# Six scratch tiles, later rope factors, a rearranged first entry and later tails in a four-layer hybrid kernel

## The chip, the cores and the metric

The kernel runs on one core of one Trainium2 chip. The metric is the device time of one execution in microseconds (us); lower is better. The four compute engines are TensorE (PE in the profile, with PEld for its weight loads), VectorE (DVE), ScalarE (ACT) and GpSimd (POOL); SP is the engine whose queue issues the DMAs.

## The reference

One sequence of 16 meta tokens and 1024 tokens, width 1024, passes through four residual layers: sliding-window attention (A), mLSTM (B), HGRN2 (C) and attention again.

```
for i in range(DEPTH):                       # kinds A, B, C, A
    u = rmsnorm(h, norm_gain[i])
    y = branch[i](u)                         # in-projection, mixer, gate, out-projection
    h = h + y

# A: 16 query heads, 4 key/value heads of 64, window of 128, blocks of 128
q, k, v, z = split(u @ w_in, (1024, 256, 256, 1024))
q = rope(rmsnorm(q, q_gain), pos); k = rope(rmsnorm(k, k_gain), pos)
o = sliding_window_attention(q, k, v, sinks)
y = (o * silu(z)) @ w_out

# C: 8 heads, per step of the scan over chunks
o     = (q * exp(A)) @ S + att(q, k, A) @ v
S_new = exp(A_last) * S + (k * exp(A_last - A)).T @ v
```

Everything is float32. A product is made of three products of fp32r parts: a high and a low part of each operand, the low-low product left out.

## The kernel before, in words

Activations lie transposed: width on the partitions in 8 slabs (KT), tokens along the free dimension in three chunks of 400, 384 and 256 columns (`CHUNKS`). `x` is the residual, `uh` and `ul` the high and low part of the normalised input. `proj` multiplies a 128-column weight slab with one chunk in 24 matmuls (8 slabs, three products) into a PSUM tile `pj`.

The program is a list of steps. Each step has a nominal PE cost, and lists are merged by these costs: `weave` mixes two lists in proportion, `later` and `spread` put a step in after so many nanoseconds of nominal PE time. That fixes PE's order of instructions as written. The other engines' orders are chosen by a scheduler, from readiness and from which buffers are free, and then run in that order. So one more buffer can change the orders of ACT, DVE, POOL and of SP's DMA queue, with PE's left alone.

Three buffers matter. `tmp()` hands out scratch tiles `t` of 128x404 from `TMPS` = 5. The rope factors `cs` (cosine and sine) have a single buffer. The ring `v` has ten tiles of 258 columns.

In the attention layers `qk_proj` handles a chunk of a query or key projection. `evac` copies the PSUM tile to `dst` (L523), squares it into `sq` (L524), and starts four DMAs that write `dst` with its halves swapped into `rot` (L527); `dst`, `sq` and `rot` are three scratch tiles for queries and for the second key slab, and rows of a larger pool for the first key slab. It first issues the DMA of the rope factors (L520). `finish` adds three delayed steps: 2000 ns later `stat`, a matmul of `sq` with a mask (L533) and two ACT steps (L361, L362); 4000 ns later `rope`, four DVE instructions (L538 to L541); 6000 ns later the split into high and low parts: L492 and L493 for queries (`q_split`), L473 to L476 for keys (`k_split`).

Normalisation (`Norm`): the 8 slabs of a chunk are squared on ACT (L377) and added up on DVE (L381), a matmul with a block of ones sums over partitions (L389), ACT forms the reciprocal root, and 8 `unit` steps make `uh` and `ul` (L415, L195, L196). In the first layer this is done chunk by chunk while the first projections run: the sums come in two halves per chunk (`PARTS`), put between the projections at fractions of their time (`FIRST`). Per chunk the head of layer one does a key slab and the first query slab; the second query slab follows for all three chunks after the third.

In layer C each of 8 heads goes through 5 regions of tokens. `level` (DVE and ACT) builds decay factors, `levels_mm` a burst of small matmuls into `pm` (L1127, L1137), `tail0` masks and sums them into `att` (DVE, POOL L1165, ACT). The tail follows while the next region's levels are made: `tail1` transposes (`pt`, L1187), `tail2` for each block does `po` (L1202 with `att`, L1204 with the state `S`) and `pa` (L1209), from which DVE makes the next `S` (L1214). `TAIL_LAG` is the nominal time by which the tail is put back before it is woven with the next region.

```
mx += weave(main[r], last)
last = [[TAIL_LAG, lambda: None, None]] + tails[r]
```

Of the kernel before, what the change touches and what calls it, by code (L numbers as in the profile page):

```python
# [30 lines left out]
    return (0, NMETA) if b == 0 else (NMETA + P * (b - 1), P)  # L31


C_IDENT, C_ONES = 0, 128
C_W = 256
# [76 lines left out]
def hybrid_kernel(ctx: ExitStack, tc: tile.TileContext, ins, out, layers=(0, 1, 2, 3)):  # L112
# [13 lines left out]
    def nm(x):  # L126
        ctr[0] += 1
        return f"{x}{ctr[0]}"
# [10 lines left out]
    def tmp():  # L139
        return tpool.tile([P, 404], F32, tag="t", name=nm("t"), bufs=TMPS)  # L140
# [12 lines left out]

    s.preload_act_table_set("natural_log_exp_and_others")

    const = cpool.tile([P, C_W], F32, name="const")
    ident = const[:, C_IDENT : C_IDENT + P]
    ones = const[:, C_ONES : C_ONES + P]
# [11 lines left out]
    def load_x(n):  # L170
        c0, cn = CHUNKS[n]
        for k in range(KT):
            sp.dma_start(x[:, k, c0 : c0 + cn], ins["xT"][k, :, c0 : c0 + cn])

    load_x(0)
    sp.dma_start(const, ins["const"])
    sp.dma_start(ngain, ins["ngain"])

    layer_pool = [None]
# [189 lines left out]
        return f  # L369

    class Norm:
        def __init__(self, i):
            self.i, self.acc, self.ps = i, {}, {}

        def sq(self, m, n, c0, cn, size=KT):
            q = tmp()[:, :cn]
            s.activation(q, x[:, m, c0 : c0 + cn], AF.Square)  # L377
            if m % size == 0:
                self.acc[n] = q
            else:  # L380
                v.tensor_tensor(self.acc[n], self.acc[n], q, op=ALU.add)  # L381

        def stat(self, n, part=0, parts=1):
            cn = CHUNKS[n][1]
# [7 lines left out]

            return [4 * cn * MM, fn, None]

        def stats(self, n, parts):

            c0, cn = CHUNKS[n]
            size = KT // parts

            def squares(part):  # L400
                def fn():
                    for m in range(part * size, (part + 1) * size):
                        self.sq(m, n, c0, cn, size)

                return [0.0, fn, None]

            return [z for k in range(parts) for z in (squares(k), self.stat(n, k, parts))]

        def unit(self, n, k):
            c0, cn = CHUNKS[n]  # L410
# [34 lines left out]
    def layer_a(i, j, first, last, fin):  # L445
# [69 lines left out]
        def qk_proj(src, gcol, work, fsplit, ch):  # L515
            late = {}

            def evac(acc, n, c0, cn):
                cos_sin = R["mix"].tile([P, 2, 400], F32, tag="cs", name=nm("cs"), bufs=1)
                sp.dma_start(cos_sin[:, :, :cn], ins["rope"][:, :, c0 : c0 + cn].rearrange("a p t -> p a t"))  # L520
                dst, sq, rot = work(n, c0, cn)
                late[n] = dst, sq, rot, cos_sin
                s.activation(dst, acc[:, :cn], AF.Identity, scale=R["cons"][:, gcol : gcol + 1])  # L523
                s.activation(sq, acc[:, :cn], AF.Square)  # L524
                for q in range(4):
                    o = q ^ 1
                    sp.dma_start(rot[32 * q : 32 * q + 32], dst[32 * o : 32 * o + 32])  # L527

            def finish(n, c0, cn):
                def stat():  # L530
                    dst, sq, rot, _ = late[n]
                    st = psa()
                    pe.matmul(st[:, :cn], R["masks"][:, 0:P], sq, start=True, stop=True)  # L533
                    rstd_from(st, sq, cn, 64)

                def rope():
                    dst, sq, rot, cos_sin = late[n]
                    v.tensor_tensor(dst, dst, cos_sin[:, 0, :cn], op=ALU.mult)  # L538
                    v.tensor_tensor(rot, rot, cos_sin[:, 1, :cn], op=ALU.mult)
                    v.tensor_tensor(dst, dst, rot, op=ALU.add)  # L540
                    v.tensor_tensor(dst, dst, sq, op=ALU.mult)  # L541
# [741 lines left out]
        return head, body, oc[5], oc[7]  # L1283

    steps = []
    norm = Norm(layers[0])

    steps += norm.stats(0, PARTS[0]) + [norm.unit(0, k) for k in range(KT)]
    tail = None
    for pos, i in enumerate(layers):  # L1290
        lastl = pos == len(layers) - 1
# [43 lines left out]
    steps[k][2]()  # L1335
    steps[k][2] = None
    load_x(1)
    k = 0
    for n, (cost, fn, pre) in enumerate(steps):
        while k < len(steps) and (k <= n or ahead < LOOKAHEAD):  # L1340
# [29 lines left out]
def _layout(inp):  # L1370
# [4 lines left out]
    const = np.zeros((P, C_W), np.float32)  # L1375
    const[:, C_IDENT : C_IDENT + P] = np.eye(P)
    const[:, C_ONES : C_ONES + P] = 1.0
    am = np.zeros((P, 384), np.float32)
    am[:64, :64] = 1.0
    am[64:, 64:128] = 1.0  # L1380
# [5 lines left out]
    f["const"] = const  # L1386
# [77 lines left out]
```

## Time and profile before

| | before |
|---|---|
| three runs | 2693.47, 2697.60, 2699.81 us |
| the profiled execution, its own time | 2690.46 us |
| its span, first to last instruction | 2688.7 us |
| layer one's entry, up to the first score matmul | 0 to 87 us |
| rest of layer A, then B, C, A | about 87 to 560, to 1560, to 2210, to the end |

A line of the timeline or of a wait names engine, source line, operation, output and inputs. A bracket at its end gives the engine's idle time just before and the instruction that ended it. PE's work is the largest, so an idle gap of PE is the first thing to look for. An idle gap on another engine matters only if PE waits for it.

### The profile page before, as it was taken

The page shows a single profiled execution, that of the slowest core. Times are in us where ns is not written, and L with a number is a line of the kernel's source. Part 1 is how long each engine was busy: PE and PEld are TensorE (multiplying, and loading weights), DVE is VectorE, ACT ScalarE, POOL GpSimd, SP SyncE. Part 2 cuts the span into 40 slices and gives each one's busy share as a digit, 9 for nine tenths or more (in the row PEclk, how much of TensorE's full clock was granted, in tenths as well). Part 3 has the DMA queues.
Part 4 walks back from the last instruction along what each step waited for, and adds up shares of the span by engine and source line. Part 5 has one row for each costly group of instructions (what it writes and reads, how often), then busy time and mean ns, then how long its engine had stood idle before and what let it go on. Part 6 is the DMA issues. An engine that isn't in the chain of part 4 may idle for free.

```text
span 2688.7 us, 54502 instructions
## 1 busy us (share of the span) xinstructions
PE 2590.5 (96%) x20276; PEld 2492.4 (93%) x20276; DVE 1959.5 (73%) x5337; ACT 1693.4 (63%) x4339; POOL 370.1 (14%) x760
## 2 busy tenths in 40 slices
PE   6899999999999999999999999999999998998999
PEld 5898989999999999999999998999999898898999
DVE  7787687974646474747475688978878978886886
ACT  7776777565454545454545657877676857766772
POOL 0343243000000000000000000101000000541450
PEclk8999999999999999999999999999999999999999
DMA  4223111011111111111111111101111013212212
GB/s 148 84 59 96 52 58 46 21 65 56 40 56 40 56 40 56 40 56 40 56 40 53 51 34 33 34 33 34 41 33 39 31 45 107 69 53 88 73 36 75
DMA packets 89786, 145.66 MB, mean 54 GB/s; under 512 B 12448, under 2 KB 42272, under 8 KB 89520
## 3 DMA queue, kind: packets, MB, share of 16 engines
q1 hardware_dynamic: 89520, 142.17, 16.9%
q8 instruction: 160, 2.62, 0.4%
q14 instruction: 106, 0.87, 0.1%
HBM read 127.28 MB, written 4.26 MB: 49 GB/s over the span
## 4 chain that ended last, share of the span: by engine, by line
PE 72%; DVE 12%; ACT 8%; issue 3%; POOL 2%; DMA 2%; SPq 0%; ACTq 0%; DVEq 0%; POOLq 0%
PE pj L262 35%; PE pj L345 14%; PE pj L307 9%; ACT Sm L633 1%; PE po L667 1%; PE pt L648 1%; PE po L890 1%; POOL Sm L637 1%; PE pa L904 1%; PE po L892 1%; DVE t L415 1%; DVE ul L196 1%; DVE Sm L630 1%; DVE x L348 1%; PE pj L303 1%
## 5 line engine op out<-in xcount | busy, mean ns | idle before, releaser
L262 PE MATMUL pj<-uh,wh 128*128 128x256 f32 (+2 forms) x2688 | 930.5, 346 | 3.4 <-ACT uh L195 3.4
L262 PE MATMUL pj<-ul,wh 128*128 128x256 f32 (+2 forms) x2688 | 871.7, 324 | 3.2 <-DVE ul L196 3.1
L262 PE MATMUL pj<-uh,wl 128*128 128x256 f32 (+2 forms) x2688 | 869.6, 324 | 0.0
L262 PEld LDWEIGHTS pj<-uh,wh 128*128 128x128 f32 x2688 | 513.4, 191 | 24.3 <-issue 6.4
L262 PEld LDWEIGHTS pj<-ul,wh 128*128 128x128 f32 x2688 | 513.7, 191 | 15.2 <-DVE ul L196 5.3
L262 PEld LDWEIGHTS pj<-uh,wl 128*128 128x128 f32 x2688 | 513.2, 191 | 0.1
L637 POOL TENSOR_SCALAR Sm<-Sm,s 128x256 f32<-128x256 f32 (+2 forms) x272 | 254.5, 947 | 410.7 <-DVE s L635 406.0
L196 DVE TENSOR_TENSOR wl<-wr,wh 128x512 fp32r<-128x512 f32 x336 | 228.7, 690 | 54.1 <-ACT wh L195 51.8
L195 ACT CAST wh<-wr 128x512 fp32r<-128x512 f32 x336 | 201.9, 616 | 97.9 <-PE pj L345 27.1
L348 DVE TENSOR_TENSOR x<-x,pj 128x384 f32<-128x384 f32 (+2 forms) x480 | 234.7, 510 | 38.8 <-PE pj L345 37.1
L345 PE MATMUL pj<-yh,wh 128*128 128x384 f32 (+2 forms) x768 | 252.9, 329 | 0.0
L345 PE MATMUL pj<-yl,wh 128*128 128x384 f32 (+2 forms) x768 | 248.0, 323 | 3.3 <-DVE yl L196 3.3
L345 PE MATMUL pj<-yh,wl 128*128 128x384 f32 (+2 forms) x768 | 246.6, 321 | 0.0
L307 PE MATMUL pj<-wh,uh 128*128 128x256 f32 x768 | 231.0, 301 | 0.0
L307 PE MATMUL pj<-wh,ul 128*128 128x256 f32 x768 | 216.4, 282 | 0.0
L307 PE MATMUL pj<-wl,uh 128*128 128x256 f32 x768 | 216.1, 281 | 0.0
L633 ACT ACTIVATE Sm<-Sm,s 128x257 f32<-128x257 f32 (+2 forms) x272 | 130.6, 482 | 84.6 <-DVE s L630 75.5
L432 DVE SCALAR_TENSOR_TENSOR t<-pj,t 128x384 f32<-128x384 f32 (+2 forms) x192 | 99.0, 515 | 107.0 <-ACT t L431 106.5
L433 ACT ACTIVATE t<-t 128x384 f32<-128x384 f32 (+2 forms) x240 | 117.8, 491 | 80.1 <-DVE t L432 79.0
L345 PEld LDWEIGHTS pj<-yl,wh 128*128 128x128 f32 x768 | 145.1, 189 | 5.7 <-DVE yl L196 5.2
L195 ACT CAST yh<-r 128x384 fp32r<-128x384 f32 (+2 forms) x120 | 57.3, 479 | 143.8 <-PE pj L345 126.2
L345 PEld LDWEIGHTS pj<-yh,wh 128*128 128x128 f32 x768 | 145.3, 189 | 1.7 <-DVE S L1214 0.3
(235 smaller groups left out, 5470.9 us busy)
## 6 DMA issues: line engine op xcount, KB each, us to landing
wr<-in_b_win SPq DMA_DIRECT2D x128, 256.0 KB, 2.9
wr<-in_a_win SPq DMA_DIRECT2D x80, 256.0 KB, 2.9
wr<-in_c_win SPq DMA_DIRECT2D x64, 256.0 KB, 2.8
cs<-in_rope SPq DMA_DIRECT2D x28, 384.0 KB, 3.3
wr<-in_a_wout SPq DMA_DIRECT2D x32, 256.0 KB, 2.7
wr<-in_b_wout SPq DMA_DIRECT2D x32, 256.0 KB, 2.7
cs<-in_rope SPq DMA_DIRECT2D x20, 256.0 KB, 2.7
t<-t SPq DMA_DIRECT2D x104, 48.0 KB, 2.2
```

The lines of the kernel that those rows point to most:

```text
L195: s.copy(h, src)
L196: v.tensor_tensor(l, src, h.bitcast(F32), op=ALU.subtract)
L262: pe.matmul(acc[:, :cn], a[:, k, :], b[:, k, c0 : c0 + cn], start=(k == 0 and i == 0), stop=(k == KT - 1 and i == 2))
L303: pe.matmul(acc[:48, :256], um[0][:, k, :], m[:, kk, :], start=(k == 0 and m is wh), stop=(k == KT - 1 and m is wl))
L307: pe.matmul(acc[:cn, :256], a[:, k, c0 : c0 + cn], m[:, kk, :], start=(k == 0 and i == 0), stop=(k == KT - 1 and i == 2))
L345: pe.matmul(acc[:, :cn], a[:, k, mc], b, start=(k == 0 and i == 0), stop=(k == 1 and i == 2))
L348: v.tensor_tensor(x[:, m, c0 : c0 + cn], x[:, m, c0 : c0 + cn], acc[:, :cn], op=ALU.add)
L415: v.scalar_tensor_tensor(u, x[:, k, cs], ngain[:, self.i, k : k + 1], self.acc[n], op0=ALU.mult, op1=ALU.mult)
L432: v.scalar_tensor_tensor(a[:, :cn], z, 0.0, a[:, :cn], op0=ALU.min, op1=ALU.subtract)
L433: s.activation(a[:, :cn], a[:, :cn], AF.Exp)
L633: s.activation(Sm[:nq, u, : nk + 1], Sm[:nq, u, : nk + 1], AF.Exp, scale=-1.0, bias=st[:nq, u : u + 1], accum_out=den[:nq, u : u + 1])
L637: g.tensor_scalar(Sm[:nq, u, :nk], Sm[:nq, u, :nk], den[:nq, u : u + 1], None, op0=ALU.mult)
```

## The change

It has five parts.

1. `TMPS` goes from 5 to 6.
2. In `qk_proj` the tile for the rope factors and its DMA move from `evac` into `stat`.
3. `TAIL_LAG` goes from 600 to 2000.
4. The head of layer one does all three projections (key, first and second query slab) for each chunk, so the second query slab no longer comes last.
5. The first norm: for chunk 0 the squares are summed in four parts of two slabs. For chunks 1 and 2 they are summed in one go, the additions on GpSimd and the sum in a row of its own; the places of these steps are new. The block of ones is written by a memset, and the identity is loaded later by its own DMA. In all layers the sum of squares of chunk 2 lies in the `v` ring and no longer in a scratch tile.

```diff
-TAIL_LAG = 600.0
+TAIL_LAG = 2000.0
-ROWS, TMPS, RAWS, YS = 8, 5, 2, 3
+ROWS, TMPS, RAWS, YS = 8, 6, 2, 3
-PARTS = 2, 2, 2
-FIRST = 0.3, 0.9, 0.3, 0.7
+PARTS = 4
+FIRST = (0.2, 0.8, 0.85), (0.2, 0.75, 0.8)
...
+    ones = cpool.tile([P, P], F32, name="ones")
+    v.memset(ones, 1.0)
...
-    sp.dma_start(const, ins["const"])
...
         def sq(self, m, n, c0, cn, size=KT):
-            q = tmp()[:, :cn]
+            if m % size:
+                q = tmp()[:, :cn]
+            elif self.row is not None and n:
+                q = self.row[:, c0 : c0 + cn]
+            else:
+                q = (vtile() if n == 2 else tmp())[:, :cn]
             s.activation(q, x[:, m, c0 : c0 + cn], AF.Square)
             if m % size == 0:
                 self.acc[n] = q
             else:
-                v.tensor_tensor(self.acc[n], self.acc[n], q, op=ALU.add)
+                (v if self.row is None or n == 0 else g).tensor_tensor(self.acc[n], self.acc[n], q, op=ALU.add)
...
             def evac(acc, n, c0, cn):
-                cos_sin = R["mix"].tile([P, 2, 400], F32, tag="cs", name=nm("cs"), bufs=1)
-                sp.dma_start(cos_sin[:, :, :cn], ins["rope"][:, :, c0 : c0 + cn].rearrange("a p t -> p a t"))
                 dst, sq, rot = work(n, c0, cn)
...
                 def stat():
-                    dst, sq, rot, _ = late[n]
+                    dst, sq, rot = late[n]
+                    cos_sin = R["mix"].tile([P, 2, 400], F32, tag="cs", name=nm("cs"), bufs=1)
+                    sp.dma_start(cos_sin[:, :, :cn], ins["rope"][:, :, c0 : c0 + cn].rearrange("a p t -> p a t"))
+                    late[n] = dst, sq, rot, cos_sin
...
-            if n == 2:
+            if first:
+                parts += [tile_of([qb[0][n]], [qb[1][n]])]
+            elif n == 2:
                 parts += [tile_of(*qb)]
...
-    norm = Norm(layers[0])
-    steps += norm.stats(0, PARTS[0]) + [norm.unit(0, k) for k in range(KT)]
+    norm = Norm(layers[0], row())
+    for k in range(PARTS):
+        steps += [norm.squares(0, k, PARTS), norm.stat(0, k, PARTS)]
+    steps += [norm.unit(0, k) for k in range(KT)]
...
-            for n, t0, t1, end in ((2, h0 + h1 * FIRST[2], h0 + h1 * FIRST[3], h0 + h1), (1, h0 * FIRST[0], h0 * FIRST[1], h0)):
-                st = norm.stats(n, PARTS[n])
-                later(seq, *((t0 + (t1 - t0) * k / len(st), z) for k, z in enumerate(st)), *norm.units(n, t1, end))
+            for n, t, h in ((2, h0, h1), (1, 0.0, h0)):
+                t0, t1, t2 = (t + z * h for z in FIRST[n - 1])
+                later(seq, (t0, norm.squares(n)), (t1, norm.stat(n)), *norm.units(n, t2, t + h))
```

Lines of the new kernel are numbered a little differently: the squares L377 are L379, the DVE and GpSimd additions L383, the copies L523 and L524 are L519 and L520, the key split L471 to L474, the stat matmul L532, layer C's `po` L1203 and L1205, `pa` L1210.

First place, the entry. On DVE before, in the stretch where chunk 1 is normalised, the additions of the squares (L381) stand between the weight splits (`wl`) and the first unit (L415):

```order
L381 TENSOR_TENSOR t_218<-t_218,t_220 128x384
L381 TENSOR_TENSOR t_218<-t_218,t_223 128x384
L381 TENSOR_TENSOR t_218<-t_218,t_226 128x384
L381 TENSOR_TENSOR t_243<-t_243,t_245 128x384
L381 TENSOR_TENSOR t_243<-t_243,t_248 128x384
L196 TENSOR_TENSOR wl_384<-wr_385,wh_383 128x512
L381 TENSOR_TENSOR t_243<-t_243,t_251 128x384
L196 TENSOR_TENSOR wl_384<-wr_389,wh_383 128x512
L415 SCALAR_TENSOR_TENSOR t_274<-x,ngain,t_243 128x384
```

On POOL now, at the start of its program, the seven additions for chunk 1 into the row `r_95`, one after the other, with some small copies of the sinks (`Sm`) among them:

```order
L383 TENSOR_TENSOR r_95<-r_95,t_232 128x384
L383 TENSOR_TENSOR r_95<-r_95,t_235 128x384
L383 TENSOR_TENSOR r_95<-r_95,t_238 128x384
L383 TENSOR_TENSOR r_95<-r_95,t_241 128x384
L628 COPY Sm_803<-cons_207 16x1
L628 COPY Sm_803<-cons_207 16x1
L628 COPY Sm_847<-cons_207 16x1 x2
L383 TENSOR_TENSOR r_95<-r_95,t_244 128x384
L383 TENSOR_TENSOR r_95<-r_95,t_247 128x384
L383 TENSOR_TENSOR r_95<-r_95,t_250 128x384
```

The six additions of two half sums left DVE and became a chain of seven on POOL, and PE's stat matmul for chunk 1 now waits for the last of them.

Second place, the end of the second key slab in the first attention layer, on ACT. Before, the square of chunk 2 (L524, out of `pj_3225`) stands four instructions behind its copy (L523), with key splits of chunk 0 (`t_3160`) between:

```order
L473 CAST r_3279<-t_3160 64x400
L523 ACTIVATE t_3256<-pj_3225,cons_194 128x256
L474 CAST r_3279<-t_3160 64x400
L476 CAST r_3280<-r_3280 64x400
L473 CAST r_3281<-t_3160 64x400
L474 CAST r_3281<-t_3160 64x400
L524 ACTIVATE t_3257<-pj_3225 128x256
L476 CAST r_3282<-r_3282 64x400
L361 ACTIVATE t_3257<-pa_3308,eps 128x256
```

On ACT now, the same chunk:

```order
L519 ACTIVATE t_3253<-pj_3224,cons_207 128x256
L520 ACTIVATE t_3254<-pj_3224 128x256
L471 CAST r_3278<-t_3159 64x400
L472 CAST r_3278<-t_3159 64x400
L358 ACTIVATE t_3254<-pa_3309,eps 128x256
L471 CAST r_3280<-t_3159 64x400
L474 CAST r_3279<-r_3279 64x400
L472 CAST r_3280<-t_3159 64x400
```

Copy and square moved ahead of all of chunk 0's key splits. PE's order is the same at both.

Third place, layer C's first head, on PE, blocks 3 and 4. Before, behind `po`, the state product and `pa` of block 3 stand six projection rows and the next region's burst (`pm`) ahead of block 4:

```order
L1202 MATMUL po_19376<-att_18665,v_18868 128x128
L1204 MATMUL po_19376<-X_19617,S_19597 128x128
L1209 MATMUL pa_19714<-v_18868,kT_19681 128x128
L262 MATMUL pj_19673<-uh,wh_19440 128x400
L262 MATMUL pj_19673<-ul,wh_19440 128x400
L262 MATMUL pj_19673<-uh,wl_19441 128x400
L262 MATMUL pj_19673<-uh,wh_19440 128x400
L262 MATMUL pj_19673<-ul,wh_19440 128x400
L262 MATMUL pj_19673<-uh,wl_19441 128x400
L1127 MATMUL pm_19724<-X_19626 32x64 x4
```

On PE now, the same two blocks, after that burst:

```order
L259 MATMUL pj_19659<-uh,wl_19448 128x400
L1203 MATMUL po_19377<-att_18666,v_18869 128x128
L1205 MATMUL po_19377<-X_19618,S_19604 128x128
L1210 MATMUL pa_19793<-v_18869,kT_19706 128x128
L1203 MATMUL po_19797<-att_18666,v_18953 128x128
L1205 MATMUL po_19797<-X_19618,S_19795 128x128
L1210 MATMUL pa_19800<-v_18953,kT_19706 128x128
L259 MATMUL pj_19804<-uh,wh_19447 128x384
```

Both blocks moved behind the burst and stand back to back here: the second state product reads the state that DVE makes from the `pa` two rows ahead.

More of the change, by code (lines that the diff above doesn't have):

```diff
@@ L31, in blk @@
     return (0, NMETA) if b == 0 else (NMETA + P * (b - 1), P)
-C_IDENT, C_ONES = 0, 128
-C_W = 256
 B_COLS = 96
 LOOKAHEAD = 12000.0
-TAIL_LAG = 600.0
+TAIL_LAG = 2000.0
 PRIO = 40
-ROWS, TMPS, RAWS, YS = 8, 5, 2, 3
+ROWS, TMPS, RAWS, YS = 8, 6, 2, 3
 XS = 14
@@ L154, in hybrid_kernel @@
     s.preload_act_table_set("natural_log_exp_and_others")
-    const = cpool.tile([P, C_W], F32, name="const")
-    ident = const[:, C_IDENT : C_IDENT + P]
-    ones = const[:, C_ONES : C_ONES + P]
+    ident = cpool.tile([P, P], F32, name="ident")
+    ones = cpool.tile([P, P], F32, name="ones")
+    v.memset(ones, 1.0)
     ngain = cpool.tile([P, 4, KT], F32, name="ngain")
@@ L371, in hybrid_kernel, with __init__ @@
     class Norm:
-        def __init__(self, i):
-            self.i, self.acc, self.ps = i, {}, {}
+        def __init__(self, i, row=None):
+            self.i, self.row, self.acc, self.ps = i, row, {}, {}
         def sq(self, m, n, c0, cn, size=KT):
-            q = tmp()[:, :cn]
+            if m % size:
[4 more added lines that the diff above has]
+                q = (vtile() if n == 2 else tmp())[:, :cn]
             s.activation(q, x[:, m, c0 : c0 + cn], AF.Square)
@@ L393, in stat, with squares, fn @@
             return [4 * cn * MM, fn, None]
-        def stats(self, n, parts):
-            c0, cn = CHUNKS[n]
+        def squares(self, n, part=0, parts=1):
             size = KT // parts
[L400 to L407, printed above, removed]
+            def fn():
+                for m in range(part * size, (part + 1) * size):
+                    self.sq(m, n, *CHUNKS[n], size)
+            return [0.0, fn, None]
         def unit(self, n, k):
@@ L518, in evac @@
             def evac(acc, n, c0, cn):
-                cos_sin = R["mix"].tile([P, 2, 400], F32, tag="cs", name=nm("cs"), bufs=1)
-                sp.dma_start(cos_sin[:, :, :cn], ins["rope"][:, :, c0 : c0 + cn].rearrange("a p t -> p a t"))
                 dst, sq, rot = work(n, c0, cn)
-                late[n] = dst, sq, rot, cos_sin
+                late[n] = dst, sq, rot
                 s.activation(dst, acc[:, :cn], AF.Identity, scale=R["cons"][:, gcol : gcol + 1])
@@ L1337, in hybrid_kernel @@
     load_x(1)
+    sp.dma_start(ident, ins["ident"])
     k = 0
@@ L1374, in _layout @@
     f["ngain"] = np.asarray(inp["norm_gain"]).reshape(4, KT, P).transpose(2, 0, 1)
-    const = np.zeros((P, C_W), np.float32)
-    const[:, C_IDENT : C_IDENT + P] = np.eye(P)
-    const[:, C_ONES : C_ONES + P] = 1.0
     am = np.zeros((P, 384), np.float32)
@@ L1385, in _layout @@
     f["b_mask"] = np.where(ii <= np.arange(P)[None], 0.0, BIG).astype(np.float32)
-    f["const"] = const
+    f["ident"] = np.eye(P, dtype=np.float32)
     half = 32
```

## The prediction

> **What bounds the kernel now.** I read the page's busy times, then the busy times by stage, then what PE waits for, then the timeline at the longest waits.
>
> ```profile
> span 2688.7 us, 54502 instructions
> PE 2590.5 (96%) x20276; PEld 2492.4 (93%) x20276; DVE 1959.5 (73%) x5337; ACT 1693.4 (63%) x4339; POOL 370.1 (14%) x760
> ```
> ```profile
> core 0: us, PE busy (x) PEld busy (x) DVE busy (x) ACT busy (x) POOL busy (x), PEclk, DMA share, GB/s
> 0.00:87.26 87.26, 60.67 (x270) 51.38 (x271) 61.49 (x127) 60.78 (x129) 1.73 (x9) 0.88 0.49 150
> 87.26:560.00 472.74, 449.00 (x2966) 430.55 (x2965) 383.96 (x1029) 327.91 (x869) 155.56 (x298) 0.98 0.18 55
> 560.00:1560.00 1000.00, 999.02 (x6584) 970.04 (x6583) 596.45 (x1526) 529.63 (x1249) 6.96 (x65) 1.00 0.15 50
> 1560.00:2210.00 650.00, 631.93 (x7514) 605.03 (x7513) 545.72 (x1697) 455.39 (x1267) 57.26 (x135) 0.99 0.11 36
> 2210.00:2689.00 479.00, 449.88 (x2948) 435.41 (x2947) 371.87 (x961) 319.66 (x826) 148.56 (x253) 0.98 0.23 71
> ```
> ```profile
> core 0: 2688.7 us, clock 0.986
> ```
>
> PE is the bound: layer B (third row) has no gap. The gaps, length minus busy, are 26.6 us in the entry, 23.7 in the rest of the first A layer, 18.1 in C and 29.1 in the last A layer. The clock of 0.986 costs at most 0.014 x 2688.7 = 37.6 us more, of which the entry has 0.12 x 87.26 = 10.5, so 27 lie behind it. Only these sums, 98 us of gaps and 38 of clock, can be won. PE's waits, first over the span, then in 88 to 560 us, then in 2210 to 2689 us:
>
> ```profile
> PE pa L533 <- ACT t L524: 37.3, 15, 4.8
> PE po L1202 <- POOL att L1165: 16.0, 10, 3.5
> ```
> ```profile
> PE pa L533 <- ACT t L524: 14.5, 4, 4.8
> ```
> ```profile
> PE pa L533 <- ACT t L524: 17.8, 8, 4.8
> PE pa L533 <- ACT r L524: 2.1, 1, 2.1
> ```
>
> So 14.5 + 17.8 + 2.1 = 34.4 us of the A layers' gaps behind the entry are one wait: the query or key statistic waits for its square. Nearly all of C's gaps is the wait for `att`.
>
> **Part 1 and 2, six scratch tiles and the later rope factors.** The longest such wait, PE, ACT and DVE, then the clock over it:
>
> ```profile
> 265.53 0.35 PE L262 MATMUL pj<-uh,wl 128*128 128x400 f32 x1
> 270.65 1.22 PE L533 MATMUL pa<-t,masks 128*128 128x256 f32 x2 [4.77 <-ACT t L524]
> ```
> ```profile
> 267.56 0.47 ACT L523 ACTIVATE t<-pj,cons 128x256 f32<-128x256 f32 x1
> 269.55 0.52 ACT L474 CAST r<-t 64x400 fp32r<-64x400 f32 x1
> 270.21 0.38 ACT L524 ACTIVATE t<-pj 128x256 f32<-128x256 f32 x1
> ```
> ```profile
> 264.82 0.57 DVE L538 TENSOR_TENSOR t<-t,cs 128x400 f32<-128x400 f32 x1
> 266.51 0.57 DVE L541 TENSOR_TENSOR t<-t,t 128x400 f32<-128x400 f32 x1
> ```
> ```profile
> 268.00:270.00 2.00, 0.00 (x0) 0.00 (x0) 0.69 (x2) 1.94 (x5) 0.00 (x0) 0.53 0.75 249
> 272.00:274.00 2.00, 2.00 (x8) 1.98 (x6) 1.29 (x3) 1.93 (x5) 0.00 (x0) 0.50 0.50 142
> 276.00:278.00 2.00, 2.00 (x15) 1.92 (x14) 0.76 (x2) 0.97 (x3) 0.00 (x0) 1.00 0.18 17
> ```
>
> The projection ended at 265.5, yet its copy came at 267.56 and its square at 270.21. In between ACT ran the key split of chunk 0 (L473 to L474): with five tiles, chunk 0's `dst` and chunk 1's three leave one, so the copy takes what chunk 0's rope lets go and the square waits until chunk 0's split has freed `dst`. In the changed order the two stand together ahead of that split, which is what a sixth tile should do. The copy still follows chunk 0's rope, which ended at 267.1. That rope was late too, for its own rotation DMAs waited for a tile and for the factors in front of them in SP's queue:
>
> ```profile
> SPq L520 <- DVE t L539: 91.3, 38, 6.1
> ```
>
> That is 2.4 us of SP's queue held at each of 38 places until the last rope has read the one buffer. With the DMA in `stat`, the rotation goes ahead of the factors where they would wait; the factors themselves come no earlier. Nothing is added but order. I take 85% of the 34.4 us, 29 us, and leave 15% for chunks of 256 columns, where a chunk's PE work is shortest and the single factor buffer serves slowest. Bounds: 34.4, and half of it, 17, if the factor buffer is the real limit.
>
> The clock rows show what a long wait costs besides: half rate (0.53, 0.50) from 268 to about 275, some 4 us of it behind the wait, which loses 2 us. The 27 us of clock behind the entry lie at such waits, those in A and C; with 85% of the waits gone and a few half-rate stretches lying in idle time, I take 20 us, 12 in A and 8 in C (bounds 8 and 24). A's sum is then 29 + 12 = 41 us (bounds 22 and 49).
>
> **Part 3, later tails in C.**
>
> ```profile
> 1668.24 0.80 PE L1202 MATMUL po<-att,v 128*128 128x128 f32 x2 [3.49 <-POOL att L1165]
> ```
>
> The ten waits of 16.0 us are at most 3.5 us long. A region takes 650 / 40 = 16 us. Its tail of some 2000 nominal ns (214 + 500 + 2 x 640) began after 600 of 2600, 23%, and now begins after 2000 of 4000, 50%: `att` gets some 4 us more; so all 16 go, and their 8 of clock. But the two blocks of a tail come closer, and the state passes through DVE between them. From the start of `pa` to the end of the new state takes 0.77 us at best, 1.50 in the mean of 64 pairs, 3.78 at worst. The worst and the last pair:
>
> ```profile
> 1824.45 0.39 PE L1209 MATMUL pa<-v,kT 128*128 128x128 f32 x2
> 2165.73 0.39 PE L1209 MATMUL pa<-v,kT 128*128 128x128 f32 x2
> ```
> ```profile
> 1827.89 0.34 DVE L1214 SCALAR_TENSOR_TENSOR S<-S,s,pa 128x128 f32<-128x128 f32 x1
> 2166.16 0.35 DVE L1214 SCALAR_TENSOR_TENSOR S<-S,s,pa 128x128 f32<-128x128 f32 x1 [0.62 <-PE pa L1209]
> ```
>
> In the changed order 32 of the 64 successions have at most 19 projection rows between them, 4 of them none and 15 six; before there are 8 with at most 12. The 32 have 263 rows between them; at 2 us for fifteen (the last clock row) they take 35 us, and with `pa` and the first `po`, some 0.3 us for each succession, the cover is about 45 us in all, 1.4 each. With each latency at the best value only the four bare ones wait, 2 us in all; with the 64 measured ones drawn at random the sum is 14; with the worst everywhere 32 x 3.78 - 45 = 76. I take 8, between the first two, since 21 of the 64 are at the best value. C's sum: 16 + 8 - 8 = 16 us (bounds 22 and, with the worst, a loss of 52).
>
> **Part 4 and 5, the entry.**
>
> ```profile
> 5.48 3.25 ACT L377 ACTIVATE t<-x 128x400 f32<-128x400 f32 x6 [0.87 <-DMA x<-in_xT]
> 21.59 2.64 ACT L377 ACTIVATE t<-x 128x384 f32<-128x384 f32 x6
> ```
> ```profile
> 8.62 3.01 PE L389 MATMUL pa<-t,const 128*128 128x400 f32 x4 [8.62 <-DMA const<-in_const]
> 24.39 0.91 PE L389 MATMUL pa<-t,const 128*128 128x384 f32 x2 [3.00 <-DVE t L381]
> 28.59 1.11 PE L389 MATMUL pa<-t,const 128*128 128x384 f32 x2
> 44.05 1.22 PE L389 MATMUL pa<-t,const 128*128 128x256 f32 x2 [4.05 <-DVE t L381]
> 82.26 1.22 PE L533 MATMUL pa<-t,masks 128*128 128x256 f32 x2 [3.90 <-ACT t L524]
> 87.26 0.17 PE L624 MATMUL pm<-r,qs 128*16 128x16 f32 x1
> ```
> ```profile
> L637 POOL TENSOR_SCALAR Sm<-Sm,s 128x256 f32<-128x256 f32 x224 | 224.6, 1014 | 208.4 <-DVE s L635 203.9 <-PE pt L648 3.8
> L637 POOL TENSOR_SCALAR Sm<-Sm,s 128x144 f32<-128x144 f32 x32 | 23.1, 733 | 128.6 <-DVE s L635 128.5
> ```
>
> The first score matmul starts at 87.26 us. PE's own work up to there is 87.3 - 26.6 - 10.5 = 50 us, so PE has 37 to give. The memset of ones takes the constants' DMA off the first statistic; the last squares end near 8.7 us anyway, so this gives about 1 us. The second query slab of chunk 0 now fills the time in which chunk 1 is normalised, that of chunk 1 the time of chunk 2, so the separate pass at the end falls away, with its wait of 3.90 us. The next limit is ACT: 60.8 us of work, which moves but does not shrink, behind a start that it spends waiting for `x` and for the first statistic, some 9 us. That puts the score matmul at 70 us at the earliest, a gain of 17.
>
> The additions are POOL's now, 14 of them, and no row shows a two-input one. The nearest rows rise by 281 ns over 112 columns, 2.5 ns a column, so one of 384 columns with one input would take 1014 + 128 x 2.5 = 1.33 us; with a second input at the same price 2.3. Seven in a row make 9.3 to 16 us, from about 22 us on, so chunk 1's sum is there at 31 to 38, against 28.6 before (its second half, third PE row). PE covers some 4 us of that with the new slab. I take 1.33, the nearest row, and the score matmul at 77 us: 10 us gained, between the bound of 17 and, with slow additions, a loss of 3. The chunk-2 sums in the `v` ring cost nothing: that tile is held while PE still has projections to run, and layer entries at 560 and 1560 lie in stages with few gaps.
>
> On such additions the Trainium skill, GPSIMD Engine Reference, section 3.1, states about 2.6 cycles per element at 1.2 GHz and 4497 ns for 2048 columns, twice VectorE's time, and in 4.1 advises against GpSimd for them. An estimate from it is 0.84 us for 384 columns; seven would take 5.9 us and the entry would gain some 3 us more. No run here shows it yet.
>
> **The sum.** Against the profiled execution: 2690.5 - 41 - 16 - 10 = 2623.5 us. That execution lies 7.1 us under the median of the three runs, so the median after is 2631 us.
>
> **Rivals.** First, POOL's chain is the entry's limit: at 2.3 us and more an addition, chunk 1's units start 6 to 7 us later, chunk 2's again, and the entry loses 3 instead of winning 10: 2644. For it: the additions run while DVE, busy 61.5 of 87 us, adds two scratch or weight tiles at a time. The page named above says in section 1 that GpSimd shares its SBUF ports with such VectorE instructions; the rows of L637, 1.0 us in a stage where DVE is 80% busy, show little of it. Against it: PE has the second query slab to run meanwhile.
>
> Second, the factor buffer, not the scratch tiles, limits the query chunks, so the change does only part of what it seems to: half the waits in A and their clock stay, 20 us less: 2651. For it: the 91.3 us of SP waits. Against it: at 270 us ACT waited for a split, not for factors.
>
> Third, slower: in C, PE waits for the state at the 32 close blocks. At a latency L for each the loss is 32 L - 45 us; it eats the other gains (41 + 24 + 10 = 75) at 3.75 us and is a measurable loss from 3.9. Two of 64 pairs came near that; if a waiting DVE delayed all that stands behind it, and L were 4.5, the time would be 2698 - 75 + 99 = 2722. Against it: the mean of 1.50.
>
> **How the numbers follow.** The forecast gets 0.64, the POOL chain 0.14, the factor buffer 0.14, the state wait 0.04, and 0.04 is left for no difference by parts that cancel. About 0.2%, 5 us, is what a measurement of this kernel can tell from no change. Faster 0.64 + 0.14 + 0.14 = 0.92, same 0.04, slower 0.04. The range: with every part at its best, 17 + 49 + 22 = 88, the median would be 2610; I go to 2606. With both milder rivals together it is 2664; I go to 2672.
>
> **What would show it.** Right: PE's wait for L524's successor falls from 37 us to under 8, that for `att` to under 2; the first score matmul near 77 us; a new wait of `po` for the state `S` of 2 to 14 us; mean clock near 0.99 or above. Wrong: POOL additions above 2 us each with a PE gap at chunk 1's statistic; waits of L533 that remain with `cs` or `t` DMAs at their head; state waits above 20 us.

## The result: 2653.0 us, 1.65% faster, by less than forecast

| | before | changed |
|---|---|---|
| median | 2698.0 us | 2653.0 us |
| range of four runs | 2693.5 to 2699.8 | 2650.3 to 2655.1 |
| profiled execution, own time (span) | 2690.5 (2688.7) | 2655.1 (2653.0) |

The ratio is 0.9835 (95%: 0.9818 to 0.9852). The gain is 45 us where 67 were forecast; the range 2606 to 2672 holds it. Between the two profiled executions only 35.7 us of span lie, because the one of before lay 7.6 us under its median and the changed one 2.1 us above; the other 9 us are not in these two traces.

The changed kernel's busy times, then its span and clock:

```profile
PE 2582.6 (97%) x20276; PEld 2482.5 (94%) x20276; DVE 1954.8 (74%) x5324; ACT 1690.5 (64%) x4339; POOL 379.5 (14%) x774
```
```profile
core 0: 2653.0 us, clock 0.992
```

Its five stages, cut at the same places of the program as those of before (length, then busy time of PE, PEld, DVE, ACT, POOL, then clock, DMA share, GB/s):

```profile
0.00:82.48 82.48, 63.61 (x270) 51.87 (x271) 57.25 (x108) 57.21 (x122) 14.60 (x23) 0.88 0.46 140
82.48:547.00 464.52, 446.19 (x2967) 427.22 (x2965) 386.49 (x1037) 329.79 (x877) 155.29 (x298) 0.99 0.20 59
547.00:1545.00 998.00, 997.82 (x6582) 968.90 (x6583) 595.53 (x1527) 529.72 (x1249) 6.96 (x65) 1.00 0.16 50
1545.00:2185.00 640.00, 627.77 (x7514) 603.23 (x7513) 542.84 (x1696) 454.36 (x1267) 55.98 (x135) 0.99 0.12 36
2185.00:2653.00 468.00, 447.18 (x2948) 431.23 (x2946) 372.72 (x961) 319.45 (x826) 146.64 (x253) 0.99 0.24 72
```

Against the lengths before, the entry is 4.8 us shorter, the rest of the first A layer 8.2, B 2.0, C 10.0 and the last A layer 11.0 (the cuts behind the entry are rounded; they sum to 36.0). PE's waits now, over the span:

```profile
PE pa L532 <- ACT t L520: 10.7, 9, 1.9
PE pj L259 <- ACT uh L192: 9.6, 7, 3.8
PE pt L647 <- POOL Sm L636: 8.8, 11, 1.7
PE pj L342 <- DVE yl L193: 8.2, 9, 2.7
PE pa L391 <- DVE t L383: 6.1, 3, 4.9
PE po L1205 <- DVE S L1215: 5.4, 11, 1.4
...
PE pm L1138 <- DVE X L1115: 2.4, 1, 2.4
...
PE pa L1210 <- ACT kT L1190: 1.2, 1, 1.2
PE pa L391 <- POOL r L383: 1.1, 1, 1.1
...
PE po L1203 <- POOL att L1166: 0.6, 1, 0.6
```

The first row was 37.3 us, the last 16.0; the last fell as forecast, the first not quite so far. The state wait is there, as forecast. The forecast left the rows between as they were. But before, PE waited 3.4 us for `uh`, 7.3 for `Sm` and 3.3 for `yl`, and not at all for `X` and `kT`. The wait of the out-projection for the low part of its gated input (`yl`) is an example. Before, over the span:

```profile
PE pj L345 <- DVE yl L196: 3.3, 6, 0.8
```

Its longest place now, in the last A layer, on PE, then ACT, then DVE:

```profile
2519.40 0.61 PE L342 MATMUL pj<-yl,wh 128*128 128x384 f32 x1 [2.74 <-DVE yl L193]
```
```profile
2515.25 0.52 ACT L192 CAST yh<-r 128x384 fp32r<-128x384 f32 x1
```
```profile
2518.47 0.40 DVE L540 TENSOR_TENSOR t<-t,t 128x256 f32<-128x256 f32 x1
2518.79 0.55 DVE L193 TENSOR_TENSOR yl<-r,yh 128x384 fp32r<-128x384 f32 x1
```

The high part was cast by 2515.8, so the low part could have followed at once. It stands on DVE behind a rope and score work, and PE waits 2.74 us. The same place before, on ACT, then DVE:

```profile
2553.06 0.51 ACT L195 CAST yh<-r 128x384 fp32r<-128x384 f32 x1
```
```profile
2555.20 0.42 DVE L541 TENSOR_TENSOR t<-t,t 128x256 f32<-128x256 f32 x1
2555.53 0.55 DVE L196 TENSOR_TENSOR yl<-r,yh 128x384 fp32r<-128x384 f32 x1
```

There too the low part stood behind a rope and score work, 2.0 us behind its cast (3.0 now), and PE came to it just in time, at 2556.14 us. But PE had waited 2.42 us for a square some 11 us earlier, and now it does not. PE comes sooner, and DVE's order does not make the low part sooner. So part of the wait for a scratch tile became a wait for VectorE's order.

### The profile page after: what moved, and what is told of

It reads as the page before. It is cut to its first block, busy times and chain, and to the rows that moved or that the text cites. A ratio compares the mean times of both kernels' runs of the same rounds, so it can differ in the third digit from the quotient of the medians.

```text
span 2653.0 us, 54472 instructions
## 1 busy us (share of the span) xinstructions
PE 2582.6 (97%) x20276; PEld 2482.5 (94%) x20276; DVE 1954.8 (74%) x5324; ACT 1690.5 (64%) x4339; POOL 379.5 (14%) x774
## 5 line engine op out<-in xcount | busy, mean ns | idle before, releaser
L636 POOL TENSOR_SCALAR Sm<-Sm,s 128x256 f32<-128x256 f32 (+2 forms) x272 | 253.2, 943 | 382.0 <-DVE s L634 364.0
L192 ACT CAST wh<-wr 128x512 fp32r<-128x512 f32 x336 | 202.1, 615 | 98.0 <-PE pj L342 26.6
```

What stands on the lines that cost most here:

```text
L192: s.copy(h, src)
L636: g.tensor_scalar(Sm[:nq, u, :nk], Sm[:nq, u, :nk], den[:nq, u : u + 1], None, op0=ALU.mult)
```

## The experiments

"Won" is the median of the kernel before, run among the same runs, less the median of the kernel.

| kernel | median us | won us | ratio and 95% interval |
|---|---|---|---|
| the whole change | 2653.0 | 45.1 | 0.9835 (0.9818 to 0.9852) |
| sixth tile alone | 2659.2 | 36.8 | 0.9868 (0.9854 to 0.9881) |
| sixth tile, later factors | 2664.1 | 31.8 | 0.9884 (0.9870 to 0.9897) |
| tail lag alone | 2683.2 | 12.8 | 0.9954 (0.9941 to 0.9968) |
| entry alone | 2690.3 | 5.6 | 0.9982 (0.9972 to 0.9991) |
| sixth tile and tail lag | 2650.5 | 45.8 | 0.9830 (0.9816 to 0.9843) |
| whole, factors early again | 2650.1 | 46.1 | 0.9828 (0.9814 to 0.9841) |
| whole, additions on DVE | 2649.0 | 47.2 | 0.9829 (0.9811 to 0.9847) |
| whole, both of these | 2646.8 | 49.5 | 0.9817 (0.9803 to 0.9830) |
| both, tail lag 1300 | 2651.2 | 44.6 | 0.9830 (0.9817 to 0.9843) |
| both, old order of projections | 2644.8 | 51.1 | 0.9806 (0.9792 to 0.9820) |
| both, half factors twice | 2642.6 | 53.3 | 0.9796 (0.9782 to 0.9809) |
| old order, tail lag 3000 | 2646.8 | 46.3 | 0.9829 (0.9816 to 0.9843) |

An interval of a ratio is some 3.5 us to either side, so a step of 2 or 3 us between two rows is not resolved by itself.

**Sixth tile alone.**

```diff
-ROWS, TMPS, RAWS, YS = 8, 5, 2, 3
+ROWS, TMPS, RAWS, YS = 8, 6, 2, 3
```

> The kernel before with TMPS = 6 and nothing else. My theory: the waits of the A layers' statistic for its square are a matter of scratch tiles, and the whole change won about 19 us there (8 in the rest of the first A layer, 11 in the last). With the sixth tile alone I expect 12 to 19 us of that, a time of 2679 to 2686 against 2698, and PE's wait for the square (37 us before) under 18. Rival, the factor buffer is the limit: under 5 us won, and the wait stays above 28.

It won 36.8 us, about twice what I expected, most of the gain of the whole change. PE's waits over its span:

```profile
PE pa L533 <- ACT t L524: 11.4, 9, 4.3
...
PE pj L345 <- DVE yl L196: 8.2, 9, 2.7
```

The wait for the square fell from 37.3 to 11.4 us, that for `att` stayed at 16.1, and the wait for `yl` rose to the very 8.2 us of the whole change. So this one line carries the change in the A layers, its benefit and its new wait. The factor buffer as the main reason for the waits is refuted.

**Sixth tile and later factors** (parts 1 and 2).

```diff
             def evac(acc, n, c0, cn):
-                cos_sin = R["mix"].tile(...)
-                sp.dma_start(cos_sin[:, :, :cn], ...)
...
                 def stat():
+                    cos_sin = R["mix"].tile(...)
+                    sp.dma_start(cos_sin[:, :, :cn], ...)
```

> The kernel before with TMPS = 6 and the rope factors' tile and DMA moved into stat (parts 1 and 2). My theory: 16 to 21 us won (2677 to 2682), PE's wait for the square near 11 as in the whole change. If the later DMA matters by itself, this stands 3 us or more below the kernel with the sixth tile alone; if it only sets an order, the two are within 2 us. Rival, the two parts give the whole 41 us forecast and another part of the change takes 20 back: 2660 or less.

31.8 us: far more than my span, far less than the 41 of the third case. Part 2 itself gained nothing: 5.0 us less was won than with the tile alone, though the intervals overlap. DVE's wait for the factors, first with the tile alone, then with both parts:

```profile
DVE t L538 <- DMA cs<-in_rope: 4.7, 4, 1.6
```
```profile
DVE t L539 <- DMA cs<-in_rope: 10.2, 8, 2.3
```

Issued later, the factors land later, and the rope waits twice as long for them. It waits less for its rotation (`t<-t`), 6.4 us instead of 9.3, so its whole delay grew by less. PE's wait for the square rose from 11.4 to 13.5 us. The second key slab of my longest wait shows how close the two orders are. DVE, ACT and PE in the changed kernel, then DVE and PE with the sixth tile alone:

```profile
255.79 0.58 DVE L537 TENSOR_TENSOR t<-t,cs 128x400 f32<-128x400 f32 x1 [2.10 <-DMA cs<-in_rope]
```
```profile
259.06 0.38 ACT L520 ACTIVATE t<-pj 128x256 f32<-128x256 f32 x1 [0.61 <-DVE t L540]
```
```profile
259.50 0.88 PE L532 MATMUL pa<-t,masks 128*128 128x256 f32 x2 [1.88 <-ACT t L520]
```
```profile
254.79 0.58 DVE L538 TENSOR_TENSOR t<-t,cs 128x400 f32<-128x400 f32 x1 [1.92 <-DMA t<-t]
```
```profile
258.50 0.70 PE L533 MATMUL pa<-t,masks 128*128 128x256 f32 x2 [1.35 <-ACT t L524]
```

The square of chunk 2 no longer waits for chunk 0's split, but it still waits for a rope's end. With late factors that rope waits 2.10 us for them; with early ones it waits 1.92 us for its rotation. In the kernel of this experiment the two waits at this place are 1.97 and 1.61 us, so late factors cost PE only some 0.3 us here.

**Tail lag alone** (part 3).

```diff
-TAIL_LAG = 600.0
+TAIL_LAG = 2000.0
```

> The kernel before with TAIL_LAG = 2000 and nothing else (part 3). My theory: layer C gives 8 to 12 us (2686 to 2690), PE's wait for att falls from 16 us to under 2, and a new wait of po for the state of 4 to 7 us appears. Rival, C's gain in the whole change comes with the sixth tile instead: within 4 us of before.

12.8 us won, slightly above my span. In its trace PE's wait for `att` is down to one of 0.6 us, and a wait of the forecast kind is new, with two that the forecast did not have:

```profile
PE po L1204 <- DVE S L1214: 5.5, 11, 1.4
...
PE pm L1137 <- DVE X L1114: 2.5, 1, 2.5
...
PE pa L1209 <- ACT kT L1189: 1.3, 1, 1.3
...
PE po L1202 <- POOL att L1165: 0.6, 1, 0.6
```

C's gain needs no sixth tile, and the waits for `X` and `kT` come with the later tails.

**Entry alone** (parts 4 and 5): the whole change with `TMPS` 5, `TAIL_LAG` 600 and the factors in `evac`.

> The kernel before with parts 4 and 5 only (three projections for each chunk, the sums of squares in parts and on GpSimd, the memset of ones); five scratch tiles, early rope factors and the old tail lag. My theory: the entry's gain does not need the sixth tile, the first score matmul comes at 81 to 84 us, 4 to 8 us won (2690 to 2694). Rival, with five tiles the denser entry stalls on scratch tiles: the first score matmul at 87 or later and nothing won. If the parts simply add up, the gains of this kernel, of the one with parts 1 and 2 and of the one with part 3 make 45 us.

5.6 us won, and the first score matmul at 84.20 us, a little behind the 81 to 84 expected, so the gain here doesn't need the sixth tile. With the 31.8 and 12.8 of the others the sum is 50.2, not 45: the parts lose some 5 us of each other's gain, with an uncertainty as large. Without part 2 the three single gains would make 55.

**Sixth tile and tail lag together**, the two diffs above and nothing else.

> The kernel before with TMPS = 6 and TAIL_LAG = 2000, nothing else. My theory: these two parts act in different layers and add up, 36.8 + 12.8 = 50 us won, 2644 to 2650, which is less time than the whole change (2653). Rival, a sixth tile and later tails share a gain in C: 2651 or more.

45.8 us won against 49.6 by addition: 2650.5 lies between my span and the rival's, and the intervals allow full addition. What matters more: two numbers give as much as the whole change, so parts 2, 4 and 5 together brought nothing that can be measured.

**The whole change with the factors early again** (the diff of part 2 backwards).

> The whole change without part 2: the rope factors' tile and DMA stand in evac again. My theory: with six tiles the later DMA is late for the rope, and moving it back wins 3 to 8 us over the whole change, 2645 to 2650; DVE's wait in L538 for the factors falls from some 12 us to near 5. Were all parts but this one to add up, it would come to 2641. Rival, the later DMA matters only where the entry is the old one: 2653 within 2 us.

2650.1, at the edge of my span, and only 1.0 us more is won than by the whole change. PE's wait for the square fell by as much, from 10.7 to 9.7 us. DVE's wait for the factors fell as expected, from 12.5 us in the whole change to

```profile
DVE t L536 <- DMA cs<-in_rope: 3.6, 4, 1.5
```

**The whole change with the additions on VectorE.**

```diff
-                (v if self.row is None or n == 0 else g).tensor_tensor(self.acc[n], self.acc[n], q, op=ALU.add)
+                v.tensor_tensor(self.acc[n], self.acc[n], q, op=ALU.add)
```

> The whole change with the first norm's additions for chunks 1 and 2 on VectorE instead of GpSimd. My theory: the GpSimd additions slow VectorE beside them and cost the entry a few us; on VectorE seven additions of some 0.45 us take 3 us instead of 7.5, but stand behind weight splits: first score matmul at 78 to 83 us, time 2649 to 2654. Rival, VectorE is the entry's scarce engine and GpSimd relieves it: first score matmul at 84 or later, 2655 or more.

2649.0, and the first score matmul came at 79.70 us instead of 82.48. First GpSimd's additions in the changed kernel (mean ns of one behind the comma), then VectorE beside those of chunk 2, then the same rope in this experiment, with the additions between:

```profile
L383 POOL TENSOR_TENSOR r<-r,t 128x384 f32<-128x384 f32 x7 | 7.5, 1066 | 22.3 <-ACT t L379 21.9
...
L383 POOL TENSOR_TENSOR r<-r,t 128x256 f32<-128x256 f32 x7 | 6.2, 886 | 17.0 <-ACT t L379 16.6
```
```profile
47.86 1.04 DVE L537 TENSOR_TENSOR t<-t,cs 128x400 f32<-128x400 f32 x1
48.83 1.10 DVE L538 TENSOR_TENSOR t<-t,cs 128x400 f32<-128x400 f32 x1
...
50.99 0.99 DVE L540 TENSOR_TENSOR t<-t,t 128x400 f32<-128x400 f32 x1
```
```profile
45.98 0.42 DVE L383 TENSOR_TENSOR r<-r,t 128x256 f32<-128x256 f32 x1
46.32 0.57 DVE L537 TENSOR_TENSOR t<-t,cs 128x400 f32<-128x400 f32 x1
...
48.78 0.57 DVE L540 TENSOR_TENSOR t<-t,t 128x400 f32<-128x400 f32 x1
```

On VectorE alone four additions and the rope took 3.4 us. With the additions on GpSimd the rope alone took 4.1. So VectorE was not relieved at this place. But most of the 2.8 us at the first score matmul was won ahead of it, at chunk 1. Its statistic came at 29.30 us instead of 31.25, without PE's wait of 1.1 us for POOL (0.7 us had been won before it), and its first projection 1.9 us earlier, at 33.04 instead of 34.92. GpSimd's additions for chunk 2 start only at 47.75 us.

**Both edits**, factors early and additions on VectorE.

> Both of these edits at once: the whole change with the rope factors' DMA back in evac and the first norm's additions on VectorE. My theory: the two gains add, 2642 to 2650. Rival: the same as with the factors alone, since in the entry only one of VectorE's late instructions decides.

2646.8: the two add, within my span. Each of these steps lies within the intervals. That part 2 lost in all three pairs (5.0, 1.0 and 2.3 us of what was won) and GpSimd in both (2.1 and 3.4) makes the sign likely, not the size. With late factors PE's wait for the square was the longer one in all three pairs too, by 2.1, 1.0 and 2.3 us.

**Tail lag 1300**, on the kernel with both edits.

> The best kernel so far (the whole change with the factors' DMA in evac and the additions on VectorE, 2646.8 us, PE's wait for the state 5.8 us, for att under 1) with TAIL_LAG = 1300 instead of 2000. My theory: tail blocks come further apart, so the wait for the state falls under 4 us, but att comes late again in some regions, 3 to 8 us of waiting; 2647 to 2653. Rival, 2000 is more than att needs and the state waits are the only price: 2642 to 2645.

The time is in my span, and 4.9 us less is won than with 2000, where the intervals still overlap. Half of my reason was wrong:

```profile
PE po L1204 <- DVE S L1214: 7.7, 8, 1.6
...
PE po L1202 <- POOL att L1165: 4.4, 6, 2.1
```

`att` is late again, but the state wait rose from 5.8 to 7.7 us instead of falling. An earlier tail does not make it smaller; why, these runs don't show.

**The old order of projections**, on the kernel with both edits (part 4 undone).

```diff
-            if first:
-                parts += [tile_of([qb[0][n]], [qb[1][n]])]
-            elif n == 2:
+            if n == 2:
                 parts += [tile_of(*qb)]
```

> The same best kernel without part 4: the second query slab comes for all three chunks after the third chunk, as before. My theory: the three projections per chunk are what the entry gained (7 us there with the additions on VectorE), so the first score matmul falls back to 84 to 88 us and the time is 2650 to 2655. Rival, VectorE sets the entry and the order of the projections does not matter: first score matmul within 2 us of 80.

The rival held as to the order: the first score matmul at 80.91 us against 80.16, and 2644.8 us, the lowest time of all kernels that compute the whole. That VectorE sets the entry is not shown by this run. Part 4, from which I had expected most of the entry's gain, gives nothing that can be measured here. PE's waits up to 90 us, with part 4 and then without:

```profile
PE pj L259 <- ACT uh L192: 9.7, 7, 3.8
```
```profile
PE pj L259 <- ACT uh L192: 6.2, 5, 2.7
```

The old order waits less for the normalised input. This kernel is also 5.3 us of gain ahead of the sixth tile and tail lag alone, which is what the rest of part 5 (sums in one row, their places, the memset), with the additions on VectorE, may be worth; the two intervals still touch.

**Half-sized factors in two buffers**, on the kernel with both edits.

```diff
-                cos_sin = R["mix"].tile([P, 2, 400], F32, tag="cs", name=nm("cs"), bufs=1)
-                sp.dma_start(cos_sin[:, :, :cn], ...)
+                cos_sin = R["mix"].tile([P, 400], F32, tag="cs", name=nm("cs"), bufs=2)
+                sp.dma_start(cos_sin[:, :cn], ins["rope"][0, :, c0 : c0 + cn])
...
-                    v.tensor_tensor(dst, dst, cos_sin[:, 0, :cn], op=ALU.mult)
-                    v.tensor_tensor(rot, rot, cos_sin[:, 1, :cn], op=ALU.mult)
+                    v.tensor_tensor(dst, dst, cos_sin[:, :cn], op=ALU.mult)
+                    v.tensor_tensor(rot, rot, cos_sin[:, :cn], op=ALU.mult)
```

> The same best kernel with half-sized rope factors in two buffers: only the cosines are loaded and both products read them, so the rope is not computed rightly; it has half the bytes and never has to wait for a single buffer. Theory: the factor buffer costs next to nothing once there are six scratch tiles; PE's wait for the square (9.1 us) stays above 7 and the time within 3 us of 2647. Rival of the prediction, the factor buffer is a limit of its own: that wait under 4 us and 2640 or less.

```profile
PE pt L646 <- POOL Sm L635: 11.4, 15, 2.6
...
PE pa L531 <- ACT t L522: 3.3, 4, 1.1
```

My theory fell on the wait, the rival on the time, which lies between the two. The wait for the square dropped from 9.1 to 3.3 us, so what the sixth tile leaves of it comes mostly from the factors' load. But only 4 us came off, at the edge of the intervals, and PE's waits for `Sm` (8.7 us without this edit) and for `t` in L579 (4.3 us against 0.7) are longer. Whether fewer bytes or the second buffer did it stays open.

**Tail lag 3000**, on the fastest version.

> The fastest full version so far (six scratch tiles, factors' DMA in evac, additions on VectorE, the old order of projections, 2644.8 us) with TAIL_LAG = 3000 instead of 2000. From 1300 to 2000 PE's wait for the state fell from 7.7 to 5.8 us and that for att from 4.4 to under 1. My theory: att has all the time that it needs at 2000, so only the state wait changes, by up to 3 us either way; 2642 to 2648. Rival, later still packs the blocks of a tail closer and the prediction's state wait comes true: above 14 us of waiting for the state and 2655 or more.

```profile
PE pa L1207 <- ACT kT L1187: 6.7, 11, 1.0
...
PE po L1202 <- DVE S L1212: 2.5, 6, 0.9
```

2646.8, and relative to before (0.9829 against 0.9806) no better than 2000. The state wait fell further, to 2.5 us, and PE waits for the transposed keys (`kT`) instead, which was 1.3. At none of the three lags tried does PE wait for nothing in C.

## Why the prediction was right, and where it was off

The sum went by one profiled execution, so it is held against the changed kernel's profiled execution.

| term | forecast | measured | from |
|---|---|---|---|
| wait for the square, behind the entry | -29 | -23 | 34.4 to 11.1 |
| wait for `att` | -16 | -15 | 16.0 to 0.6 |
| new state wait | +8 | +5 | 0 to 5.4 |
| clock behind the entry | -20 | -11 | PE busy 2529.8 to 2519.0 |
| all other gaps behind the entry | 0 | +13 | rest of 71.6 to 51.5 |
| entry | -10 | -5 | 87.26 to 82.48 |
| sum | -67 | -36 | |

*Right.* PE's waits were the right place to look. The mechanism of part 1 held at its longest place: that wait fell from 4.77 to 1.88 us, and the square stands ahead of the split. Over the span the wait stopped at 11.1 us and not under 8, and at that place one sign of being wrong is there, a rope that waits for a `cs` DMA. In C the two named waits went as said: `att` under 2 us, the state between 2 and 14. The slower rival's latency of 3.9 us was not reached: from the start of `pa` to the end of the new state it was 3.06 us at worst and 1.39 in the mean of the 64 pairs, and 1.4 us was the longest single wait.

*The step that failed most* is the unspoken one: that a wait taken away shortens the program by its length. The named waits fell by 33 us and PE's gaps by 20. Of the 13 us in between, 9.6 are in the A layers and 4.2 in C (B has 0.8 less). `yl` has 4.9 of it, level factors (`X`) 2.4, `Sm` 1.5 and `kT` 1.2. I named what is late next only for the state in C, where I had counted distances. In A I named nothing, where I ought to have asked what PE would come to next, sooner than before. The sixth tile alone brought the same 8.2 us of `yl`, the tail lag alone the waits for `X` and `kT`.

*Clock.* I took 20 of 27 us as lost work that would come back. The mean clock did reach 0.992, a rise of 0.006 or some 16 us of span, but PE's busy time behind the entry fell by 10.8. Summed over the clock records of the two traces, half rate behind the entry cost 27.5 us before, 24.4 of them while PE worked, and 12.2 now, 11.8 of them while PE works. So the term was nearly twice too large mainly because 12 us of half rate stayed. Only 2.8 us of what went had lain in gaps, where it costs nothing. Seven stretches of 3.4 us at half rate are left behind the entry, and four of them lie at waits that the forecast did not name: for `kT`, `X`, `Sm` and, here, `yl`.

```profile
2519.50:2522.90 3.40, 3.40 (x14) 3.30 (x15) 2.85 (x6) 1.64 (x4) 2.06 (x4) 0.50 0.00 0
```

*Part 2* was "nothing but order", so it had no price of its own. It moves a load 2000 nominal ns later on a path where the rope waits for it. I looked at what stands behind the DMA in SP's queue and not at who waits for the load. The runs put it at a loss of 1 to 5 us, each within the intervals.

*The factor buffer as a rival*: refuted as the main limit (the sixth tile won 36.8 us by itself), but the factors' load is behind most of the wait for the square that is left (5.8 of 9.1 us went with half the bytes and two buffers). That 2653 lies next to this rival's 2651 is chance. Between the two profiled executions the A stages became 19.2 us shorter, where 41 were forecast and 21 would be left with this rival, but not for its reason.

*Entry.* The bound was to be ACT, and the gain was to come from the second query slab in the gaps. The runs bear out neither. Taking that slab's new place back moved the first score matmul by 0.75 us. PE's gaps in the entry fell by 7.7 us, from 26.6 to 18.9, but the same 270 matmuls kept PE busy 2.9 us longer. The memset took away the wait of 8.62 us for the constants, but not the 1 us that I had given it: the first projection matmul came at 14.07 us instead of 14.11. PE's longest wait for `uh` now is for chunk 1's last unit:

```profile
46.20 0.69 PE L259 MATMUL pj<-uh,wh 128*128 128x384 f32 x1 [3.77 <-ACT uh L192]
```
```profile
43.74 0.56 DVE L540 TENSOR_TENSOR t<-t,t 128x400 f32<-128x400 f32 x1
44.22 0.60 DVE L413 SCALAR_TENSOR_TENSOR t<-x,ngain,r 128x384 f32<-128x384 f32 x1
```

That unit stands on DVE behind the end of the first chunk's second rope (and before it, from 40.2 us on, behind the rest of both ropes and a key split). There are seven waits for `uh`, 9.6 us, against 3.4 us before; the longest is 3.8 with the additions on either engine, and 2.7 with the old order of projections. With five tiles (entry alone) the longest is 2.7 too, and PE waits 1.8 us for a square (L522) near this place. So part 4 and the sixth tile together filled one gap with PE work and opened another. That the ropes brought forward are the reason is likely from DVE's order but not shown, because the old order also has chunk 1's statistic 2.1 us earlier (27.47 instead of 29.55 us).

*POOL.* The chain was not the limit that the rival had: at 1.07 us an addition was cheaper than my 1.33, and PE waited 1.1 us for the last. Still, with the additions on VectorE chunk 1 came 1.9 us earlier, and that is most of what they won in the entry. The estimate from the Trainium skill, GPSIMD Engine Reference, section 3.1 (0.84 us) was nearer to 1.07 than mine, from below. That estimate goes by columns alone. With VectorE idle, an addition of 384 columns took 1.00 us and one of 256 columns 0.73, which is 2.1 ns a column and some 0.2 us for each instruction. The advice of the Trainium skill, GPSIMD Engine Reference, section 4.1, against such additions fits the 2.1 and 3.4 us that they lost here. What the Trainium skill, GPSIMD Engine Reference, says in section 1, that GpSimd shares its SBUF interfaces with VectorE instructions that have two SBUF inputs, fits VectorE's slower rope (0.99 to 1.10 us an instruction against 0.57).

*The median.* Before's profiled execution was 7.1 us quicker than its median; I added that to the result. The changed kernel's was not quicker than its own, so 9 us of the 45 come from which executions were profiled. Without that the sum was 31 us too large, not 22. To that extent the nearness of 2631 to 2653 is luck; the range would have held about 2662 too.

## What to carry to other kernels

When a wait of the bounding engine goes, ask what that engine comes to next, and which engine makes it in which order; here 33 us less of the named waits came with 13 us of others. Try the parts of a change alone: two constants gave as much as the whole change. Before giving an addition to GpSimd, look at which VectorE instructions will run beside it and at who waits for the end of the chain, and before delaying a load, look at who waits for it.

## What the runs showed of the hardware

- Two-input VectorE instructions of 400 columns took 0.99 to 1.10 us beside GpSimd additions and 0.57 without them. Beside GpSimd's one-input multiplications (L636) seven such rope instructions took 0.57 to 0.60 us. The page's row of busy time shows none of this as waiting; it shows only as longer instructions.
- A GpSimd addition of 384 columns took 0.99 to 1.01 us while VectorE was idle (four of the seven) and 1.11 and 1.34 us beside VectorE. One of 256 columns took 0.73 us while VectorE was idle (entry alone, at 52.89 us) and up to 0.96 beside it; the same 256 columns took VectorE 0.42 us.
- Half rate came in stretches of 3.4 us or twice that. In the changed kernel one followed a PE wait of only 1.2 us (at 1645.1 us), while a wait of 1.85 us (at 360.3 us) had none.
- Kernels with an identical entry reached the first score matmul at 87.26 us (before) and at 85.40 (tail lag alone), with a mean clock of 0.88 and 0.94 up to there. So 2 us at that mark can be chance, and of the entry's 4.8 us less than half may be.
